# Two up-projection blocks run as one at the entry of a feed-forward layer, with the residual's pieces made on demand

## The chip, the cores and the metric

The kernel runs on one core of one Trainium2 chip. The metric is device time of one execution in microseconds (us), as the median of several runs. Profiles are of one execution.

## The reference

A decoder layer on 256 tokens of width 2048, in float32: two token mixers with a gated merge, cross-attention into 256 memory tokens, and a feed-forward layer with a causal convolution. Each is wrapped in norms. What matters here is the seam between the second and the third:

```python
x = x + rms_norm(cross_attention(h, m, ...), xattn_post_norm[l])
h = rms_norm(x, ffn_pre_norm[l])
x = x + rms_norm(conv_glu_ffn(h, ffn_w_up[l], ...), ffn_post_norm[l])

def conv_glu_ffn(h, w_up, conv_w, conv_b, w_down):
    u = h @ w_up                                    # 2048 x 16384
    uc = conv_b + sum(conv_w[j] * shift_right(u, CONV_WIDTH - 1 - j) for j in range(CONV_WIDTH))
    gate, up = split_cols(uc, (D_FF, D_FF))
    return (jax.nn.gelu(gate, approximate=True) * up) @ w_down
```

## The kernel before

**Products in three parts.** Activations lie with features on the 128 partitions and the 256 tokens along the free axis: `x` is 16 tiles (k) of 128 x 256. Each operand of a large product is split into a rounded high part and the rest (`hi`, `lo`), and a product is three matmuls: high weight by high input, high weight by low input, low weight by high input (L432 to L434: `wh` with `xh`, `wh` with `xl`, `wl` with `xh`).

**Blocks and chunks.** The weights are read once, as chunks of 512 KB (128 x 1024 f32). `Feed` (L320) takes each chunk through three steps: SP loads it into `raw` (L335, three buffers), ACT makes `wh` (L360, four buffers), DVE makes `wl` (L381, four buffers). `run` (L393) goes through a list of blocks in order. A block of the up-projection is 512 columns: 8 chunks, each with two k-tiles and four groups of 128 columns, so 24 matmuls a chunk and 192 a block. It accumulates in two PSUM banks, which its evacuation (`fu_evac`, L1491) later turns into 2 x 128 rows of the gated activation `ac`. There are 32 such blocks (L1539), and two pools of four banks, `acc` and `aux`.

**The order of the work.** Every engine executes its instructions in the order written. `run` writes, at chunk i: a round of side work (`side.half`), the request for the input tile (`b["xs"](k)`, L421), `wh` and `wl` up to chunk i+3 (`feed.lo(i + 3)`, L422), the load up to chunk i+6, and then the matmuls. Side work (evacuations, statistics, transposes) is given as generators to `Spread` (L71), which advances them piece by piece within a budget of ACT and DVE time; `need` and `until` advance a generator at once.

**The residual.** Between two sublayers `Residual` (L1214) makes the new `x` and the next input. Its row of factors comes from the sum of squares of the previous output (`st`, `stb`: small matmuls on PE). Then come eight pieces of two tiles each: on DVE `z` times the factors (`scale`) and `xr` plus `z` (`add`), on ACT the high part `fh`, on DVE the low part `fl` (`parts`). The first piece works tile by tile (256 columns), the others on both tiles (512 columns), one step ahead: `scale` and `add` of piece i+1 stand in front of `parts` of piece i. It is a generator too. In the feed-forward layer it stands in the budgeted list, and `tile(k)` (L1294) also asks for three pieces from the start, always two beyond the one of tile k. Cross-attention uses the same class with `early=True` and the names `qh`, `ql`. After piece 6 the squares of the new `x` are summed (`stf`), for the factors which the evacuation applies; the `xt` transposes (L1571) start with the first evacuation.

Of the kernel before, what the change touches and what calls it, by code (L numbers as in the profile page):

```python
# [15 lines left out]
P = 128  # L16
D = 2048
S = 256
# [52 lines left out]
class Spread:  # L71
# [23 lines left out]
    def add(self, gen, chain=0, phase=0, back=False, ahead_of=None):  # L95
        s = {"gen": gen, "done": False, "gap": chain, "next": self.tick + phase}
        if ahead_of in self.back:
            self.back.insert(self.back.index(ahead_of), s)
        else:
            (self.chains if chain else self.back if back else self.bulk).append(s)  # L100
        return s

    def half(self):
        self.tick += 1
# [42 lines left out]
def _layer(ctx, tc, nc, d, dbg):  # L147
    act, dve = Meter(nc.scalar, 200.0, 0.83), Meter(nc.vector, 130.0, 1.04)
    pool, pe, sp = nc.gpsimd, nc.tensor, nc.sync
    side = Spread(act, dve)  # L150
# [30 lines left out]
    def mm(out, lhsT, rhs, start=True, stop=True):  # L181
        pe.matmul(out, lhsT, rhs, start=start, stop=stop, skip_group_check=True)  # L182
# [128 lines left out]

    blocks = []

    def block(kind, srcs, xs, evac, before=None, cols=512, pool_=None, pre=None, bankwise=False, tail=0):

        blocks.append(dict(kind=kind, srcs=srcs, xs=xs, evac=evac, before=before, cols=cols,
                           pool=pool_ or acc, pre=pre, task=None, bankwise=bankwise, tail=tail))
        return blocks[-1]

    class Feed:  # L320
# [72 lines left out]
    def run():  # L393
        feed = Feed()
        for c in range(8):
            x_load(c)
            feed.dma(c)
        i = 0
        pend = []
        for b in blocks:  # L400
            if len(pend) >= 2:
                side.need(pend[-2])
            if b["before"]:
                b["before"]()
            nm = b["cols"] // P
            if b["kind"] == "fm":
                banks = [b["pool"]("fm", [P, 2, S]) for _ in range((nm + 1) // 2)]
            else:
                banks = [b["pool"]("tm") for _ in range(2 * (b["cols"] // 512))]
            nk = sum(s.shape[1] for s in b["srcs"])  # L410
            k = 0
            nt = len(b["srcs"]) if b["bankwise"] else b["tail"]
            if nt:
                b["srcs"], tail = b["srcs"][:-nt], b["srcs"][-nt:]
            for ci, s in enumerate(b["srcs"]):
                if b["pre"]:
                    b["pre"](ci, feed)
                feed.lo(i + 1)
                side.half()
                side.more = lambda: feed.hi(i + 2)  # L420
                ahead = b["xs"](k)  # L421
                feed.lo(i + 3)  # L422
                feed.dma(i + 6)
                wh, wl = feed.st.pop(i)
                for kj in range(s.shape[1]):
                    xh, xl = b["xs"](k) if kj else ahead
                    first, last = k == 0, k == nk - 1
                    if b["kind"] == "fm":
                        for m in range(nm):
                            o = banks[m // 2][:, m % 2]  # L430
                            a, c = wh[:, kj, m * P:(m + 1) * P], wl[:, kj, m * P:(m + 1) * P]
                            mm(o, a, xh, start=(first and m % 2 == 0), stop=False)  # L432
                            mm(o, a, xl, start=False, stop=False)
                            mm(o, c, xh, start=False, stop=last)  # L434
                            if nm == 8 and m == 3:
                                side.half()
                    else:
                        for g, o in enumerate(banks):
                            tm_products(o, g * P * 512 // b["cols"], g * 512 % b["cols"], (wh[:, kj], wl[:, kj], xh, xl),
                                        first, last)  # L440
                            if len(banks) == 4 and g == 1:
                                side.half()
                    k += 1
                    if kj + 1 < s.shape[1]:
                        side.half()
                i += 1
            if nt:

                feed.lo(i + nt - 1)
                steps = []  # L450
                for s in tail:
                    w = feed.st.pop(i)
                    for kj in range(s.shape[1]):
                        steps.append((w[0][:, kj], w[1][:, kj]) + tuple(b["xs"](k)))
                        k += 1
                    i += 1
                for g, o in enumerate(banks):
                    for si, (wh, wl, xh, xl) in enumerate(steps):
                        if b["kind"] == "tm":
                            tm_products(o, g * P * 512 // b["cols"], g * 512 % b["cols"], (wh, wl, xh, xl), False,  # L460
                                        si == len(steps) - 1)
                        for m in range(2 if b["kind"] == "fm" else 0):
                            c = slice((g * 2 + m) * P, (g * 2 + m + 1) * P)
                            mm(o[:, m], wh[:, c], xh, start=(b["bankwise"] and si == 0 and m == 0), stop=False)
                            mm(o[:, m], wh[:, c], xl, start=False, stop=False)
                            mm(o[:, m], wl[:, c], xh, start=False, stop=si == len(steps) - 1)
                        if si % 2:
                            side.half()
                    if g == 0:
                        feed.lo(i + 1)  # L470
                feed.dma(i + 4)
            b["task"] = side.add(b["evac"](banks))
            pend.append(b["task"])
# [740 lines left out]
    class Residual:  # L1214


        def __init__(self, st, key, st2, hi, lo, gname, early):
            self.a = (st, key, hi, lo, gname)
            self.early, self.stats = early, None
            self.st2, self.ready = st2, 0  # L1220
            self.task = side.add(self.run(), chain=2 if early else 0)

        def run(self):
            st, key, hi, lo, gname = self.a
            z, xr = M[key], M["xr"]
            for _ in range(10):
                if st.done:
                    break
                yield
            while not st.done:  # L1230
                side._piece(side.bulk[0])
            if not self.early:
                keep_warm(2)
            rb = st.row()
            if not self.early:
                keep_warm(4)

            def parts(i, js=(0, 1)):
                for j in js:
                    k = i * 2 + j  # L1240
                    act.activation(hi[:, k], part(xr, i)[:, j], AF.Identity, scale=pcol(gname, k))
                for j in js:
                    k = i * 2 + j
                    dve.scalar_tensor_tensor(lo[:, k], part(xr, i)[:, j], pcol(gname, k), hi[:, k],
                                             op0=ALU.mult, op1=ALU.subtract)
                self.ready = i + 1

            def scale(i):
                dve.tensor_mul(part(z, i), part(z, i), bc(rb, 2))

            def add(i):
                dve.tensor_add(part(xr, i), part(xr, i), part(z, i))

            if self.early:
                yield
            a, x = part(z, 0), part(xr, 0)
            for j in range(2):
                dve.tensor_mul(a[:, j], a[:, j], rb)
            for j in range(2):
                dve.tensor_add(x[:, j], x[:, j], a[:, j])  # L1260
            scale(1)
            parts(0)
            yield
            for i in range(1, 8):
                if i == 1:
                    add(1)
                if i < 7:
                    scale(i + 1)
                    add(i + 1)
                parts(i)  # L1270
                if i == 1 and not self.early:
                    side.more()
                if i == 6:
                    self.stats = side.add(self.squares(), chain=1)
                yield
# [16 lines left out]
            side.need(self.stats)  # L1292

        def tile(self, k):  # L1294
            n = min(k // 2 + 3, 8)
            side.until(self.task, lambda: self.ready >= n)
            return self.a[2][:, k], self.a[3][:, k]

# [237 lines left out]
            return M["res"].tile(k)  # L1536
        return xs

    for b in range(32):  # L1539
        fu = block("fm", W("w_fu", b), fu_xs(b), fu_evac(b),  # L1540
              before=start_ffn if b == 0 else None, pool_=aux if b == 2 else acc)

    M["as"] = {}

# [197 lines left out]
```

## Time and profile before

| what | value |
|---|---|
| median of three runs | 1906.09 us (1905.71 to 1906.88) |
| the profiled execution | 1904.21 us |
| its span, first to last instruction | 1902.4 us |
| granted clock of TensorE | 0.999 |
| L381 DVE `wl`, 640 times | 1224 ns each |
| L360 ACT `wh`, 640 times | 1048 ns each |
| PE matmuls on `fh`, `fl` (up-projection) | 3 x 2048 |
| loads of `w_fu` | 256 of 512.0 KB, 4.2 us to landing (median) |

PE is TensorE's matmuls and PEld its weight loads, DVE VectorE, ACT ScalarE, POOL GpSimd; SP issues the loads. Rows of a timeline give start, duration, engine, line, operation, output and inputs, and in brackets the idle time of the engine before the row and what ended it. Rows of the windows give length, and busy time and instruction count of each engine. Matmuls overlap in the pipe: a row of 0.28 us is followed by the next one's start after 0.11 us.

### The profile page before, as it was taken

What the parts mean: (1) busy time and instruction counts of PE and PEld (TensorE: products, weight loads), DVE (VectorE), ACT (ScalarE), POOL (GpSimd) and SP (SyncE); (2) the same over time, 40 slices, a digit from 0 to 9 for tenths busy, and PEclk for the clock granted to TensorE, in tenths of its full rate; (3) what the DMA queues carried; (4) which work ended last, traced back from release to release, by engine and by line L of the source; (5) the groups of instructions that cost most, each with busy time, mean ns of one, the idle gap of its engine ahead of it and who ended that gap; (6) DMA issues with size and microseconds to landing.
All of it is one profiled execution on the core that took longest, in us unless ns stands there. A gap on an engine that the chain in (4) does not pass through costs nothing.

```text
span 1902.4 us, 36482 instructions
## 1 busy us (share of the span) xinstructions
PE 1881.1 (99%) x15076; PEld 1780.3 (94%) x15076; DVE 1304.6 (69%) x1836; ACT 999.7 (53%) x1438; POOL 32.1 (2%) x53
## 2 busy tenths in 40 slices
PE   9999999999999999989999999999999999999998
PEld 9999987999999999789999999999999998888886
DVE  6888975665765767678666776666776675556555
ACT  6676355544544655566555554545544454555453
POOL 0100000100100000000000000000000000000000
PEclk9999999999999999999999999999999999999999
DMA  7655554354556664536556655665556666555554
GB/s 249 183 183 181 167 163 144 110 169 144 182 178 203 234 239 167 166 117 195 192 189 194 195 189 193 197 196 192 188 193 200 194 194 212 193 197 195 193 190 154
DMA packets 97910, 352.72 MB, mean 185 GB/s; under 512 B 11056, under 2 KB 11312, under 8 KB 97360
## 3 DMA queue, kind: packets, MB, share of 16 engines
q1 hardware_dynamic: 96496, 348.07, 56.2%
q8 instruction: 118, 1.93, 0.4%
q0 software_dynamic: 384, 1.18, 0.3%
q10 hardware_dynamic: 864, 1.15, 0.2%
q14 instruction: 48, 0.39, 0.1%
HBM read 347.73 MB, written 2.10 MB: 184 GB/s over the span
## 4 chain that ended last, share of the span: by engine, by line
PE 93%; DVE 3%; DMA 2%; ACT 1%; issue 1%; POOL 0%; DVEq 0%; POOLq 0%; ACTq 0%
PE fm L182 65%; PE tm L182 24%; DVE wl L381 1%; DMA raw<-in_w_in_dram 1%; PE gram L182 0%; PE Y L182 0%; PE lv L182 0%; DVE fl L66 0%; ACT wh L360 0%; DMA x<-in_x_dram 0%; PE num L182 0%; DVE z L66 0%; PE U L182 0%; PE X L182 0%; PE zwa L182 0%
## 5 line engine op out<-in xcount | busy, mean ns | idle before, releaser
L381 DVE TENSOR_TENSOR wl<-raw,wh 128x1024 fp32r<-128x1024 f32 x640 | 779.6, 1224 | 437.0 <-ACT wh L360 434.6
L360 ACT CAST wh<-raw 128x1024 fp32r<-128x1024 f32 x640 | 669.2, 1048 | 526.2 <-PE fm L182 367.5
L182 PE MATMUL fm<-fh,wl 128*128 128x256 f32 x2048 | 566.3, 277 | 2.6 <-DVE wl L381 2.6
L182 PE MATMUL fm<-fh,wh 128*128 128x256 f32 x2048 | 567.1, 277 | 1.3 <-ACT fh L66 0.8
L182 PE MATMUL fm<-fl,wh 128*128 128x256 f32 x2048 | 566.2, 276 | 0.4 <-DVE fl L66 0.4
L182 PEld LDWEIGHTS fm<-fh,wl 128*128 128x128 f32 x2048 | 384.8, 188 | 3.2 <-DVE wl L381 3.2
L182 PEld LDWEIGHTS fm<-fh,wh 128*128 128x128 f32 x2048 | 384.7, 188 | 1.6 <-ACT fh L66 1.0
L182 PEld LDWEIGHTS fm<-fl,wh 128*128 128x128 f32 x2048 | 384.7, 188 | 0.8 <-DVE fl L66 0.8
L182 PE MATMUL tm<-wh,as 128*128 128x512 f32 x1024 | 315.2, 389 | 0.0
L182 PE MATMUL fm<-hh,wh 128*128 128x256 f32 x1072 | 302.7, 282 | 1.2 <-ACT wh L371 1.2
L182 PE MATMUL fm<-hh,wl 128*128 128x256 f32 x1072 | 298.3, 278 | 1.7 <-DVE wl L381 1.5
L182 PE MATMUL fm<-hl,wh 128*128 128x256 f32 x1072 | 297.9, 278 | 0.0
L182 PEld LDWEIGHTS tm<-wh,as 128*128 128x128 f32 x1024 | 192.2, 188 | 39.9
L182 PEld LDWEIGHTS fm<-hh,wh 128*128 128x128 f32 x1072 | 201.8, 188 | 3.9 <-ACT hh L66 1.5
L182 PEld LDWEIGHTS fm<-hh,wl 128*128 128x128 f32 x1072 | 201.7, 188 | 2.7 <-DVE wl L381 2.4
L182 PEld LDWEIGHTS fm<-hl,wh 128*128 128x128 f32 x1072 | 201.8, 188 | 0.2
L182 PE MATMUL tm<-wl,as 128*128 128x512 f32 x512 | 199.2, 389 | 0.0
L182 PEld LDWEIGHTS tm<-wl,as 128*128 128x128 f32 x512 | 96.1, 188 | 19.8
L66 ACT CAST as<-ac 128x256 fp32r<-128x256 f32 x128 | 45.6, 404 | 111.7 <-PE tm L182 111.7
L66 DVE TENSOR_TENSOR as<-ac,as 128x256 fp32r<-128x256 f32 x128 | 48.6, 421 | 60.8 <-ACT as L66 60.8
L182 PE MATMUL fm<-mgh,wh 128*128 128x256 f32 x256 | 71.1, 278 | 0.0
L182 PE MATMUL fm<-mgh,wl 128*128 128x256 f32 x256 | 70.9, 277 | 0.0
(363 smaller groups left out, 2147.8 us busy)
## 6 DMA issues: line engine op xcount, KB each, us to landing
raw<-in_w_fu_dram SPq DMA_DIRECT2D x256, 512.0 KB, 4.2
raw<-in_w_in_dram SPq DMA_DIRECT2D x160, 512.0 KB, 3.6
raw<-in_w_fd_dram SPq DMA_DIRECT2D x128, 512.0 KB, 4.2
raw<-in_w_br_dram SPq DMA_DIRECT2D x32, 512.0 KB, 3.9
raw<-in_w_mo_dram SPq DMA_DIRECT2D x32, 512.0 KB, 4.0
raw<-in_w_xk_dram SPq DMA_DIRECT2D x8, 512.0 KB, 4.4
raw<-in_w_xq_dram SPq DMA_DIRECT2D x8, 512.0 KB, 3.6
raw<-in_w_xv_dram SPq DMA_DIRECT2D x8, 512.0 KB, 4.2
```

The source lines that it names most:

```text
L66: return f(out, *a, **k)
L182: pe.matmul(out, lhsT, rhs, start=start, stop=stop, skip_group_check=True)
L360: nc.scalar.copy(wh, r)
L381: nc.vector.tensor_sub(wl, r, self.st[self.nl][0])
```

## The change

The first two blocks of the up-projection become one block of 16 chunks, which alternate between the two: chunk 0 of block 0, chunk 0 of block 1, chunk 1 of block 0, and so on. It holds four banks and is evacuated once, block 0 first (`fu_evac2`). For the very first k-tile the four products with the low part of the input come after the eight others. The feed-forward residual leaves the budgeted list: only `tile(k)` advances it, and it asks for one piece beyond the one of tile k instead of two. In both residuals the first piece alternates `mul` and `add` by tile, and its high and low parts stand ahead of `scale(1)`.

```diff
+    def own(self, gen):
+
+        return {"gen": gen, "done": False}
...
-                banks = [b["pool"]("fm", [P, 2, S]) for _ in range((nm + 1) // 2)]
+                banks = [b["pool"]("fm", [P, 2, S]) for _ in range((nm + 1) // 2 * (1 + b["two"]))]
...
-            nk = sum(s.shape[1] for s in b["srcs"])
+            nk = sum(s.shape[1] for s in b["srcs"]) // (1 + b["two"])
...
             for ci, s in enumerate(b["srcs"]):
+                second = b["two"] and ci % 2
+                if second:
+                    k -= s.shape[1]
...
                         for m in range(nm):
-                            o = banks[m // 2][:, m % 2]
+                            o = banks[second * 2 + m // 2][:, m % 2]
                             a, c = wh[:, kj, m * P:(m + 1) * P], wl[:, kj, m * P:(m + 1) * P]
                             mm(o, a, xh, start=(first and m % 2 == 0), stop=False)
-                            mm(o, a, xl, start=False, stop=False)
+                            if not (b["two"] and ci == 0 and first):
+                                mm(o, a, xl, start=False, stop=False)
                             mm(o, c, xh, start=False, stop=last)
-                            if nm == 8 and m == 3:
-                                side.half()
+                        if b["two"] and ci == 0 and first:
+
+                            for m in range(nm):
+                                mm(banks[m // 2][:, m % 2], wh[:, kj, m * P:(m + 1) * P], xl, start=False, stop=False)
...
-            self.task = side.add(self.run(), chain=2 if early else 0)
+            if early:
+                self.task = side.add(self.run(), chain=2)
+            else:
+                self.task = side.own(self.run())
...
             for j in range(2):
                 dve.tensor_mul(a[:, j], a[:, j], rb)
-            for j in range(2):
                 dve.tensor_add(x[:, j], x[:, j], a[:, j])
+            parts(0)
             scale(1)
-            parts(0)
             yield
...
         def tile(self, k):
-            n = min(k // 2 + 3, 8)
+            n = min(k // 2 + (3 if self.early else 2), 8)
             side.until(self.task, lambda: self.ready >= n)
...
+    def fu_evac2(ps):
+        for b in range(2):
+            yield from fu_evac(b)(ps[b * 2:b * 2 + 2])
+
+    block("fm", [w for c in zip(W("w_fu", 0), W("w_fu", 1)) for w in c], fu_xs(0), fu_evac2, before=start_ffn, two=True)
+    for b in range(2, 32):
+        fu = block("fm", W("w_fu", b), fu_xs(b), fu_evac(b), pool_=aux if b == 2 else acc)
```

`nm` is four in all these blocks, so the removed `side.half` was never reached.

More of the change, by code (lines that the diff above doesn't have):

```diff
@@ L312, in _layer, with block @@
     blocks = []
-    def block(kind, srcs, xs, evac, before=None, cols=512, pool_=None, pre=None, bankwise=False, tail=0):
+    def block(kind, srcs, xs, evac, before=None, cols=512, pool_=None, pre=None, bankwise=False, tail=0,
+              two=False):
         blocks.append(dict(kind=kind, srcs=srcs, xs=xs, evac=evac, before=before, cols=cols,
-                           pool=pool_ or acc, pre=pre, task=None, bankwise=bankwise, tail=tail))
+                           pool=pool_ or acc, pre=pre, task=None, bankwise=bankwise, tail=tail, two=two))
         return blocks[-1]
@@ L1537, in fu_xs @@
         return xs
-    for b in range(32):
-        fu = block("fm", W("w_fu", b), fu_xs(b), fu_evac(b),
-              before=start_ffn if b == 0 else None, pool_=aux if b == 2 else acc)
+    def fu_evac2(ps):
[4 more added lines that the diff above has]
+        fu = block("fm", W("w_fu", b), fu_xs(b), fu_evac(b), pool_=aux if b == 2 else acc)
     M["as"] = {}
```

## The prediction

> **What bounds the kernel now.** I read the page first, then the windows around the entry of the up-projection and the chain of waits there, then the timelines of PE, DVE and ACT.
>
> ```profile
> PE 1881.1 (99%) x15076; PEld 1780.3 (94%) x15076; DVE 1304.6 (69%) x1836; ACT 999.7 (53%) x1438; POOL 32.1 (2%) x53
> ...
> PE 93%; DVE 3%; DMA 2%; ACT 1%; issue 1%; POOL 0%; DVEq 0%; POOLq 0%; ACTq 0%
> ```
>
> PE is busy 99% of the span and carries 93% of the chain that ends last, so only PE's matmuls and the few places where it waits can be worth anything. The 3% of DVE in the chain is the clue: somewhere PE follows DVE. The windows give blocks 0 and 1 of the up-projection, and block 6 as the standard (length, then busy time and count of PE, PEld, DVE, ACT, POOL, then clock, DMA share, GB/s):
>
> ```profile
> 837.24:864.61 27.37, 23.91 (x192) 22.76 (x193) 26.85 (x44) 18.56 (x31) 0.00 (x0) 1.00 0.37 119
> 864.61:889.10 24.49, 24.11 (x211) 23.94 (x210) 18.27 (x27) 14.19 (x18) 0.70 (x1) 1.00 0.59 195
> ...
> 979.24:1001.01 21.77, 21.77 (x195) 21.77 (x193) 15.11 (x21) 10.90 (x14) 0.00 (x0) 1.00 0.59 195
> ```
>
> A block is 192 matmuls, 8 chunks of 24 (counts take in two or three from the edges). It takes 21.77 us when nothing stops it: 0.1134 a matmul, 2.72 a chunk. Block 0 takes 27.37, with DVE busy for 26.85 of it; block 1 takes 24.49. Together 51.86 against 43.54: **8.32 us over**. At the entry DVE is the bound: it owes one piece of the residual and one `wl` per chunk.
>
> PE's timeline shows where the 8.32 goes:
>
> ```profile
> 837.24 0.38 PE L182 MATMUL fm<-fh,wh 128*128 128x256 f32 x1 [0.83 <-ACT fh L66]
> 838.02 0.38 PE L182 MATMUL fm<-fl,wh 128*128 128x256 f32 x1 [0.40 <-DVE fl L66]
> ...
> 844.39 0.38 PE L182 MATMUL fm<-fh,wl 128*128 128x256 f32 x1 [0.53 <-DVE wl L381]
> ...
> 850.89 0.39 PE L182 MATMUL fm<-fh,wl 128*128 128x256 f32 x1 [0.44 <-DVE wl L381]
> ...
> 854.10 0.38 PE L182 MATMUL fm<-fh,wh 128*128 128x256 f32 x1 [0.43 <-ACT wh L360]
> ...
> 856.26 0.38 PE L182 MATMUL fm<-fh,wl 128*128 128x256 f32 x1 [1.66 <-DVE wl L381]
> ...
> 867.97 0.58 PE L182 MATMUL st<-ones,stf 128*128 128x1 f32 x4 [0.38 <-DVE stf L66]
> ```
>
> and the chain of waits has the small matmuls of block 1:
>
> ```profile
> 867.97 0.58 PE st L182 x4
> ...
> 871.47 0.44 PE stb L182 x4
> ...
> 874.75 0.44 PE xt L1581 x4
> ...
> 886.08 0.44 PE xt L1581 x4
> ```
>
> The five waits inside block 0 (0.40, 0.53, 0.44, 0.43, 1.66) add to 3.46. Each costs more than its bracket: from 837.24 to 838.02 PE loses 0.78 - 0.11 = 0.67, 0.27 over the bracket, since a row is drawn longer than the spacing; and the matmul after a restart is another 0.11 late. So 3.46 + 5 x 0.38 = **5.4 us**. `st`, `stb` and two `xt` take 0.58 + 3 x 0.44 = 1.9, and `st` waits 0.38 besides. That leaves 0.6: a slightly wider spacing of the matmuls.
>
> ```profile
> 856.60:864.96 8.36, 8.36 (x73) 1.00 0.65 213
> 1002.00:1010.36 8.36, 8.36 (x76) 1.00 0.54 182
> ```
>
> In windows of one length, at full clock and without an idle slot, 73 matmuls stand where 76 stand later: 4% of 2.72, 0.11 us a chunk. The wide spacing runs from the restart at 856.26 to the first `xt`.
>
> **The change part by part.** The profiled execution took 1904.21 us (span 1902.4 and 1.8 around it), 1.9 under the median 1906.09. I work out the difference inside the span and take it from the median.
>
> *Chunks in turn.* Blocks 0 and 1 become 16 chunks, so each piece (two k-tiles) feeds two chunks, 5.44 us of PE. DVE's rows at the entry give its prices:
>
> ```profile
> 835.55 0.75 DVE L66 TENSOR_TENSOR z<-z,stb 128x256 f32<-128x256 f32 x2 [1.58 <-PE stb L182]
> 836.22 0.75 DVE L66 TENSOR_TENSOR xr<-xr,z 128x256 f32<-128x256 f32 x2
> 836.89 0.68 DVE L66 TENSOR_TENSOR z<-z,stb 128x512 f32<-128x512 f32 x1
> 837.49 0.88 DVE L66 SCALAR_TENSOR_TENSOR fl<-xr,par,fh 128x256 fp32r<-128x256 f32 x2
> 838.28 0.69 DVE L66 TENSOR_TENSOR xr<-xr,z 128x512 f32<-128x512 f32 x1
> 838.88 0.68 DVE L66 TENSOR_TENSOR z<-z,stb 128x512 f32<-128x512 f32 x1
> 839.60 0.69 DVE L66 TENSOR_TENSOR xr<-xr,z 128x512 f32<-128x512 f32 x1
> 840.21 0.87 DVE L66 SCALAR_TENSOR_TENSOR fl<-xr,par,fh 128x256 fp32r<-128x256 f32 x2
> 841.00 0.68 DVE L66 TENSOR_TENSOR z<-z,stb 128x512 f32<-128x512 f32 x1
> ...
> 843.12 2.35 DVE L381 TENSOR_TENSOR wl<-raw,wh 128x1024 fp32r<-128x1024 f32 x2
> 845.39 0.68 DVE L66 TENSOR_TENSOR z<-z,stb 128x512 f32<-128x512 f32 x1
> ```
>
> A piece is 838.88 to 841.00, 2.12; a `wl` is (845.39 - 843.12)/2 = 1.14. Before: 2.12 + 1.14 = 3.26 per chunk against PE's 2.72, so PE has to stall. After: 2.12 + 2 x 1.14 = 4.40 per 5.44. DVE has 1.04 to spare in each pair of chunks, if its work comes in the right order.
>
> *Order at the entry.* `z` and `xr` now alternate by half tile. A step that reads what the step just before it wrote starts 0.72 after it (838.88 to 839.60), an independent one 0.61 (839.60 to 840.21): 0.11 more. Independent 256-wide steps stand 0.335 apart (0.67 for two). So: z 835.55, xr 836.00, z 836.33, xr 836.78 (ending 837.19), `fl` from 837.11.
>
> ```profile
> 836.67 0.91 ACT L66 ACTIVATE fh<-xr,par 128x256 fp32r<-128x256 f32 x2 [2.62 <-DVE xr L66]
> ...
> 839.82 1.03 ACT L360 CAST wh<-raw 128x1024 fp32r<-128x1024 f32 x1
> ```
>
> `fh` began 0.45 after its `xr` (836.22), PE 0.57 after that. Now `fh` begins at 836.45 and PE at 837.02, **0.2 earlier**. The eight products without `fl` come first and last to 838.0, and `fl` is there at 837.6: the wait at 838.02 goes. The second half of `fh` starts only at 837.2 and ends at 837.7, so DVE loses another 0.26 before the second `fl`. It is free at 838.17 with `z` of piece 1 still to do; its `xr` follows at 838.9, 0.6 later than before.
>
> [...]
>
> *Every deadline.* In the changed program DVE does p0, p1, `wl2` `wl3` `wl4`, p2, `wl5` `wl6`, p3, `wl7` `wl8`, p4 and so on (p is a piece; chunks 0 and 1 are staged already). Adding the prices: p1 ends at 841.7, `wl2` 842.85, `wl3` 844.0, `wl4` 845.1, p2 847.2. PE begins chunk 1 at 839.85, 2 at 842.6, 3 at 845.3, 4 at 848.0, then each 2.72. `wl2` is wanted 0.23 into chunk 2, at 842.8: a tie, for which I take 0.2 (between 0 and the 0.53 + 0.38 of the wait at 844.39, nearer to 0). `wl3` and `wl4` are 1.5 and 3 early, p2 0.8.
>
> *The weights' transfers.* There are three raw buffers, so a transfer starts when the `wl` three chunks before it ends. First SP's waits, then the transfers issued at 844.40 and at 845.50, each in a window of its own:
>
> ```profile
> SPq L335 <- DVE wl L381: 47.1, 14, 13.4
> ```
> ```profile
> raw<-in_w_fu_dram SPq DMA_DIRECT2D x1, 512.0 KB, 3.5
> ```
> ```profile
> raw<-in_w_fu_dram SPq DMA_DIRECT2D x1, 512.0 KB, 4.3
> ```
>
> SP waits for DVE 14 times. Of two transfers 1.1 apart the first lands in 3.5, the second in 4.3, 1.9 after the first. Chunk 5's now starts at 842.9 and lands at 846.4, chunk 6's at 844.0 to 848.3, chunk 7's at 845.1 to 850.2, later ones in 4.3. With 1.03 for `wh` and 1.2 for `wl`: `wl5` ends at 848.8, `wl6` 850.7, p3 852.8, `wl7` 853.9, `wl8` 855.4, p4 857.5, `wl9` 858.6, `wl10` 860.5, p5 862.6. PE wants chunk 5 at 851, p3 at 853.7, p4 at 859.1, p5 at 864.5: at least 0.9 early each time. **No further stall.** ACT has 2 x 1.03 + 0.91 in 5.44 and hides.
>
> *What only moves.* `st` now stands behind 396 matmuls instead of 216, with `stb` and the `xt` after it; the counts stay, so their 1.9 is paid later, in full. The `st` wait of 0.38 should go: the fold of `stf` follows `wl18`, due more than a chunk before. The evacuations of both blocks now run together, from chunk 18 on. One is 15.11 - 8 x 1.14 = 6.0 of DVE, and each later block leaves DVE 21.77 - 15.11 = 6.7 idle, so two blocks hide the one that is behind. I cost it at nothing; without that cover it is up to 6.0.
>
> *The first residual* (cross-attention) gets the same new order, under a saturated DVE:
>
> ```profile
> 737.92 0.87 DVE L66 SCALAR_TENSOR_TENSOR ql<-xr,par,qh 128x256 fp32r<-128x256 f32 x2
> 738.98 1.23 DVE L381 TENSOR_TENSOR wl<-raw,wh 128x1024 fp32r<-128x1024 f32 x1 [0.19 <-ACT wh L360]
> ```
> ```profile
> PE st L182 <- DVE stx L66: 1.5, 1, 1.5
> ```
>
> Two dependent steps and the wait for `fh` delay it by 0.5; the idle 0.19 takes up part. Between 0 and 0.5 reaches the `st` for which PE already waits 1.5. I take 0.2, near 0.5 less the idle and the `wh` that shifts with it.
>
> **Sum.** Gains: 5.4, 0.4 (`st`), 0.2 (start). Costs: 0.2 (first residual), 0.1 (the restart after the first matmul), 0.2 (chunk 2). The wide spacing cost 0.6; it may now cost 0 to 1.7 (16 chunks at 0.11), and I take 0.7. Net **5.4 us**: 1904.2 - 5.4 = 1898.8 for the profiled execution, **1900.7** as a median. What follows is PE's work and shifts as a whole.
>
> **The rivals.** (1) *Transfers land late together.* If the three in flight share the bandwidth evenly, 1.57 MB at the 195 GB/s of block 1's row last 8.1 us, and all land near 851. Then `wl5` is ready at 853.2 instead of 851 and p3 is pushed 0.5 past its chunk; with restarts 3 us of the gain go: 1903.7. Against it stand the 3.5 and 4.3 above. [...]
>
> (2) *The tie of chunk 2 returns at each pair.* The pieces are in truth not made only when asked for: one is queued a pair ahead, in front of the next `wl`, on an engine that works in order. Seven times 0.6 is 4.2: gain 1.2, time 1904.9. For it: the small margin of p2, 0.8. Against: DVE gains 1.04 each pair.
>
> (3) *Slower: the wide spacing stays.* Without stalls nothing interrupts PE until `st`. If PE keeps the spacing of 856 to 865, it pays 0.11 a chunk: from 55 chunks on the gain is gone, from 90 on the kernel is slower by 0.2%, and over all 256 chunks of the up-projection it is 28 us, 1928. For it: before, it lasted 18 us and through `st` and `stb`. Against: it ended at an `xt`, eight groups of `xt` follow here too, and block 6 shows no trace of it.
>
> **How the numbers follow.** The forecast has 0.70, from 1899.4 (no wide spacing, no tie) to 1902.3 (both in full); transfers 0.15; ties 0.09; spacing 0.06. A measurement of this kernel tells about 0.2%, 3.8 us, from no change: the forecast is faster by more than that (below 1902.3), (1) and (2) lie within it, (3) is slower. So faster 0.70, same 0.24, slower 0.06. The range, 1899.2 to 1904.2, takes in (1) and leaves out (2) and (3).
>
> **What would show it.** Right: the first matmul 1.5 us after the first `z` (1.7 now); the merged block's 384 matmuls in 44 to 45.5 us; no wait of PE on `wl` over 0.5, none on `fl`; `st` without a wait; `xt` still 32. (1) would show as ACT's `wh` waiting for DMA and PE for `wl` near 851; (2) as six or seven waits of PE on `wl` or `fl` at even chunks; (3) as 73 matmuls instead of 76 in 8.36 us late in the up-projection. I am wrong at the root if PE, free of DVE here, loses the time again before block 6.

## The result and the profile after

The changed kernel takes **1900.48 us** in the median of six executions, the kernel before on the same chip 1907.22. One of the six took 3822.03 us at a granted clock of 1.0, for a reason that nothing here shows, and is left out of the ratio: **0.9964 [0.9954, 0.9975]**, which is 6.9 us faster (4.8 to 8.8). The profiled execution took 1898.43 us (span 1896.7) against 1904.21 (1902.4), so 5.78 less in the two profiles.

The page of the kernel after, its busy times and the shares of the chain that ended last:

```profile
PE 1879.7 (99%) x15076; PEld 1780.6 (94%) x15076; DVE 1305.0 (69%) x1836; ACT 1000.2 (53%) x1438; POOL 32.1 (2%) x53
...
PE 93%; DVE 3%; ACT 2%; issue 1%; DMA 1%; POOL 0%; SPq 0%; DVEq 0%; POOLq 0%; ACTq 0%
```

The counts of matmuls and of DVE's and ACT's instructions are the same, and DVE's busy time differs by 0.4 us: no work went, it was put in another order. The 3% of DVE in the chain hardly answer, because 6 us are 0.3% of a span and the shares are rounded to whole per cents. The stage itself answers. Windows of the kernel after: blocks 0 and 1 as one (384 matmuls from the first), then blocks 2 to 5 with what moved into them, then block 6 as the standard (length, busy time and count of PE, PEld, DVE, ACT, POOL, then clock, DMA share, GB/s):

```profile
837.22:881.26 44.04, 44.04 (x384) 43.89 (x385) 40.20 (x56) 27.91 (x40) 0.00 (x0) 1.00 0.59 189
881.26:973.35 92.09, 92.09 (x811) 92.09 (x809) 66.29 (x96) 51.97 (x71) 0.70 (x1) 1.00 0.58 185
973.35:995.11 21.76, 21.76 (x194) 21.76 (x193) 15.03 (x21) 10.90 (x14) 0.00 (x0) 1.00 0.59 194
```

and the row of the kernel before for its blocks 2 to 5:

```profile
889.10:979.24 90.14, 90.14 (x794) 90.14 (x793) 60.84 (x82) 46.74 (x62) 0.00 (x0) 1.00 0.60 191
```

In the first row PE's busy time equals the length: it doesn't stop once. The two blocks took 51.86 before and take 44.04 now, 7.82 less. The next stretch takes 92.09 instead of 90.14, 1.95 more, with 17 matmuls more in it (four rows of four, and one at the edge): `st`, `stb` and two `xt` were inside blocks 0 and 1 and now stand behind them. DVE does 5.45 us more there, the evacuation that was put off, and PE's busy time is still equal to the length. So 7.82 - 1.95 = 5.87, and 0.02 from the start (837.22 against 837.24): block 6 begins at 973.35 instead of 979.24, **5.89 earlier**. The last matmul of the up-projection ends the same 5.89 earlier.

The chain of waits of the kernel after, at the entry and at the end of the merged block, shows the same without the sums:

```profile
835.74 0.43 DVE z L66
836.18 0.02 issue
836.20 0.44 DVE xr L66
836.64 0.02 issue
836.66 0.52 ACT fh L66
837.18 0.04 issue
837.22 45.56 PE fm L186 x396
882.78 0.34 PE st L186 x4
883.12 2.94 PE fm L186 x24
886.06 0.44 PE stb L186 x4
886.50 2.75 PE fm L186 x24
889.25 0.44 PE xt L1599 x4
```

One `z`, one `xr`, one half of `fh`, then 396 matmuls in a single step of the chain: nothing of DVE stands between them any more. `st` follows directly, with no wait.

The groups of the page that read `fh`, before and after (out<-in, shapes and count, then busy time, mean ns of one, then idle time of PE just before them and its releaser), say it for the whole up-projection. After:

```profile
L186 PE MATMUL fm<-fh,wl 128*128 128x256 f32 x2048 | 565.8, 276 | 0.0
L186 PE MATMUL fm<-fh,wh 128*128 128x256 f32 x2048 | 566.6, 277 | 0.6 <-ACT fh L66 0.6
L186 PE MATMUL fm<-fl,wh 128*128 128x256 f32 x2048 | 565.3, 276 | 0.0
```

The 0.6 is the first matmul's wait for `fh`; ahead of no other product of the up-projection's blocks is PE idle. One wait is too short to show as idle time of PE: the weight loads (PEld) of the products on `wl` wait for it for 0.2 us in all, which is the tie at chunk 2 below.

### The profile page after: what moved, and what is told of

The parts are those of the page before. It is cut to its first block, busy times and chain, and to the rows that moved or that the text cites. A ratio compares the mean times of both kernels' runs of the same rounds, so it can differ in the third digit from the quotient of the medians.

```text
span 1896.7 us, 36486 instructions
## 1 busy us (share of the span) xinstructions
PE 1879.7 (99%) x15076; PEld 1780.6 (94%) x15076; DVE 1305.0 (69%) x1836; ACT 1000.2 (53%) x1438; POOL 32.1 (2%) x53
## 4 chain that ended last, share of the span: by engine, by line
PE 93%; DVE 3%; ACT 2%; issue 1%; DMA 1%; POOL 0%; SPq 0%; DVEq 0%; POOLq 0%; ACTq 0%
PE fm L186 65%; PE tm L186 24%; DVE wl L387 1%; ACT wh L366 1%; PE gram L186 0%; PE Y L186 0%; PE lv L186 0%; DMA raw<-in_w_in_dram 0%; DVE ql L66 0%; DMA wsm<-in_w_sm_dram 0%; DVE z L66 0%; PE num L186 0%; PE U L186 0%; ACT hh L66 0%; PE X L186 0%
```

## The experiments

The theory: **DVE's load per matmul of PE** decides. At the entry DVE owed 3.26 us for each 2.72 of PE, and taking chunks in turn makes it 4.40 for each 5.44; but only if DVE also *does* its work in that order, for which the demand is needed. The rivals: the order alone, or the demand alone, or the new order of the first piece is the real cause. The first four kernels take the parts apart, the next three load DVE to find the point at which it decides, and the last changes one detail at the entry. What is moved to later blocks is paid there, so besides blocks 0 and 1 I give the time from the first matmul to the start of block 6: 142.00 us in the kernel before (27.37 + 24.49 + 90.14), 136.13 in the changed one (44.04 + 92.09), with the same matmuls in it everywhere.

**1. Chunks in turn, alone** (residual, its requests and the order of its first piece as before; the `block` lines are against the kernel before, the `if` against the changed one)

```diff
+    block("fm", [w for c in zip(W("w_fu", 0), W("w_fu", 1)) for w in c], fu_xs(0), fu_evac2, before=start_ffn, two=True)
+    for b in range(2, 32):
...
-                            if not (b["two"] and ci == 0 and first):
+                            if True:
                                 mm(o, a, xl, start=False, stop=False)
...
             self.task = side.add(self.run(), chain=2 if early else 0)
...
             n = min(k // 2 + 3, 8)
```

> Blocks 0 and 1 interleaved as in the changed kernel, all else as before: the residual in the budgeted list, three pieces from the start, old order of the first piece and of the first products. Theory (what counts is the order in which DVE gets its work, and the interleaving only makes room for it): in the program DVE's steps stand exactly as before (p0 p1 p2, wl2 wl3, p3 p4, wl4, p5 p6, wl5, p7, wl6), so wl4 and wl5 end when they ended before, 850.9 and 856.2, and PE, which reaches chunks 4 and 5 at 848.0 and 853.6 now, waits for them as before. The 384 matmuls take about 51 us less the st, stb and xt that moved out (1.9 and 0.4): 49 to 49.5. Time within 1 us of before. Rival (interleaving alone feeds PE): the 384 matmuls in 44 to 45 us and 5 us faster.

Measured: 1907.55 against 1905.93, ratio 1.0006 [0.9996, 1.0016]. Windows of this kernel, its blocks 0 and 1 in halves:

```profile
839.23:866.31 27.08, 23.30 (x193) 22.31 (x193) 26.36 (x43) 18.14 (x31) 0.00 (x0) 1.00 0.36 116
866.31:891.25 24.94, 24.07 (x207) 23.89 (x205) 14.57 (x16) 9.88 (x10) 0.70 (x1) 1.00 0.66 212
```

Together 52.02, as before (51.86), with 12 small matmuls in it instead of 16: only one group of `xt` moved out. `st` did not move behind the two blocks, as I had assumed, since the residual was finished as early as before; it waits 0.9 for `stf` in this kernel. Up to block 6 it is 142.70, which is 0.70 more than before. PE merely waits for other things. Rows of its timeline:

```profile
852.88 0.38 PE L186 MATMUL fm<-fh,wl 128*128 128x256 f32 x1 [0.77 <-DVE wl L387]
...
856.09 0.39 PE L186 MATMUL fm<-fh,wh 128*128 128x256 f32 x1 [0.43 <-ACT wh L366]
...
858.25 0.38 PE L186 MATMUL fm<-fh,wl 128*128 128x256 f32 x1 [1.66 <-DVE wl L387]
```

The last is the 1.66 of the kernel before, to the digit. DVE's instructions are the same ones in the same order: three pieces, two `wl`, then twice two pieces and one `wl`. PE needs half as many pieces in a block, but DVE makes them at the old rate all the same, in front of the `wl` that PE is waiting for. **The order of the chunks alone is worth nothing.**

**2. The demand, alone** (blocks 0 and 1 apart)

```diff
-            self.task = side.add(self.run(), chain=2 if early else 0)
+            if early:
+                self.task = side.add(self.run(), chain=2)
+            else:
+                self.task = side.own(self.run())
...
-            n = min(k // 2 + 3, 8)
+            n = min(k // 2 + (3 if self.early else 2), 8)
```

> Only the residual on demand: out of the budgeted list, two pieces from the start, one ahead of need; blocks 0 and 1 one after the other and the old order of the first piece and first products. Theory: DVE still owes 3.26 us per chunk against PE's 2.72, but the wl now alternate with the pieces (p0 p1 wl2 wl3 p2 wl4 p3 wl5 ... wl8 p7), so the waits become small and many and the last is p7's, at 835.55 + 8 x 2.12 + 7 x 1.14 + 0.1 = 860.6, where PE began chunk 7 at 861.8 before. Block 0 takes 25.5 to 26.5 us instead of 27.4; 1 to 2 us faster than before. Rival (making pieces on demand is the gain): block 0 in 22 to 23 us and 5 us faster.

Measured: 1904.70 against 1905.93, 0.9993 [0.9984, 1.0003], a difference that the interval doesn't separate from none. The windows of blocks 0 and 1, and PE's waits in block 0 (in total, times, longest):

```profile
837.13:863.48 26.35, 23.75 (x192) 22.55 (x193) 26.04 (x42) 18.18 (x30) 0.00 (x0) 1.00 0.45 142
863.48:886.89 23.41, 23.41 (x207) 23.41 (x205) 16.20 (x23) 12.87 (x17) 0.70 (x1) 1.00 0.61 192
```
```profile
PE fm L186 <- DVE fl L66: 2.6, 6, 1.4
PE fm L186 <- ACT fh L66: 0.8, 1, 0.8
```

Block 0 is 26.35 instead of 27.37, DVE busy for 26.04 of it, which is 8 x 3.26 = 26.1. The waits on `wl` have become waits on `fl`: pieces and weights keep their prices, and DVE is still the bound in block 0. Block 1 has no wait and one group of `xt` less. Up to block 6 it is 140.37, which is 1.63 less than before.

**3. The new order of the first piece, alone** (`mul` and `add` in turn, its parts ahead of `scale(1)`, the products with `fl` last)

```diff
...
                 dve.tensor_mul(a[:, j], a[:, j], rb)
-            for j in range(2):
                 dve.tensor_add(x[:, j], x[:, j], a[:, j])
-            scale(1)
             parts(0)
+            scale(1)
```

> Only the order at the entry: mul and add alternate by half tile in the first piece of both residuals with its parts ahead of scale(1), and the first k-tile's low-input products come after the eight others; blocks one after the other, residual in the budgeted list. Theory: PE starts 0.2 earlier and has no wait at its second matmul, but DVE falls 0.6 behind and every later wait of PE is on DVE, so the 0.9 comes back at chunk 2 and wl5 ends 0.6 later; with 0.2 in cross-attention the kernel is 0.6 to 1 us slower. Rival (the entry's order is part of the gain by itself): 0.9 us faster.

Measured: 1907.91 against 1905.93, 1.0011 [1.0001, 1.0020]: slightly slower. Block 0 takes 29.53. A new wait stands in chunk 1, in PE's timeline:

```profile
843.26 0.38 PE L182 MATMUL fm<-fl,wh 128*128 128x256 f32 x1 [0.79 <-DVE fl L66]
```

The wait for `wl` of chunk 5 ended 20.71 us after the first `z` before and ends 21.33 after it here: 0.62 later, which is the 0.6 by which the prediction said that DVE falls behind at the entry. The rest of the 2.2 was not expected; windows of PE alone show it (length, PE, clock, DMA share, GB/s):

```profile
854.00:858.70 4.70, 2.66 (x22) 1.00 0.34 112
858.70:859.80 1.10, 1.04 (x8) 0.95 0.21 41
859.80:863.20 3.40, 3.40 (x18) 0.51 0.80 259
863.20:870.00 6.80, 6.80 (x61) 1.00 0.62 193
```

For 3.4 us the granted clock is 0.51, with 18 matmuls where 30 fit at 0.1134. That is 12 x 0.113 = 1.4 us. So this profile shows the theory's 0.6 and a loss by the clock that I had not forecast; how much of the slower median is the clock, the times don't tell.

**4. All but the new order of the first piece** (the edits of 1 and 2 together)

> The changed kernel without its order at the entry: interleaved blocks and the residual on demand, but the old order of the first piece in both residuals and of the first products. Theory: PE starts 0.2 later and waits 0.7 at its second matmul, but DVE is 0.6 ahead, so chunk 2 has no wait, and cross-attention is 0.2 shorter: 384 matmuls in 44.3 to 44.8 us, 0.2 to 0.7 us slower than the changed kernel, some 5 us faster than before. Rival (the order at the entry carries a good part): 1.5 us or more slower than the changed kernel.

Measured: 1901.47 against 1905.93, 0.9974 [0.9964, 0.9983]. Windows of its two halves:

```profile
841.23:864.62 23.39, 22.98 (x193) 22.79 (x193) 21.03 (x30) 13.63 (x20) 0.00 (x0) 1.00 0.55 179
864.62:886.47 21.85, 21.85 (x194) 21.85 (x193) 18.71 (x26) 14.22 (x20) 0.00 (x0) 1.00 0.60 191
```

Together 45.24, which is 6.62 under before, and less the 1.95 that is paid later 4.67. Nearly the whole gain is here, from two edits of which alone, up to block 6, one lost 0.70 us and the other gained 1.63. **They need each other**: the chunks in turn make room on DVE, and the demand lets the `wl` use it. The changed kernel's 44.04 is 1.2 less. Of it 0.67 is the second matmul's wait for `fl`, and 0.75 is spacing: here the 192 matmuls of chunks 0 to 7 stand 0.1178 apart instead of 0.1134, in the changed kernel they don't. Against it stand 0.23 at chunk 2, where this kernel has no wait. The spacing is what puts 45.24 over the 44.3 to 44.8 that I had expected. The medians (0.9974 and 0.9964, intervals overlapping) don't separate this 1.2.

**5. The changed kernel with the low part made twice** in pieces 2 to 7: 0.79 more on DVE per pair of chunks, the same values written again

```diff
+                for j in js * (0 if self.early or i < 2 else 1):
+                    k = i * 2 + j
+                    nc.vector.scalar_tensor_tensor(lo[:, k], part(xr, i)[:, j], pcol(gname, k), hi[:, k],
+                                             op0=ALU.mult, op1=ALU.subtract)
```

> The changed kernel; DVE computes the low part of pieces 2 to 7 of the feed-forward residual twice (0.79 us more a piece, the same values), so a pair of chunks asks 5.19 of DVE against PE's 5.44. Theory (DVE's share of a pair is what decides): it still fits; where DVE waited for weights it works instead, and the 384 matmuls take 44.0 to 44.6 us, the time within 1 us of the changed kernel. Rival (the margin is in truth used up by the transfers and the small lead of the pieces): a wait of PE at each pair, 384 matmuls in 47 us or more.

Measured: 1901.54 against 1906.89, 0.9971 [0.9962, 0.9981]. Its two halves:

```profile
841.07:863.32 22.25, 22.25 (x193) 22.25 (x193) 21.61 (x35) 12.68 (x18) 0.00 (x0) 0.98 0.51 163
863.32:885.25 21.93, 21.93 (x194) 21.93 (x193) 21.55 (x33) 15.20 (x23) 0.00 (x0) 1.00 0.62 192
```

DVE is busy for 43.16 of 44.18 us, and PE still doesn't stop. 4.40 + 0.79 = 5.19 is under 5.44: in the merged block the work is free. The clock of 0.98 is a stretch at half clock around the first two matmuls (838.45 to 841.86), which costs 0.38 and hides the 0.23 at chunk 2; that is the 0.14 over 44.04. Up to block 6 it is 136.76, 0.63 more than in the changed kernel, since the matmuls around `st` come 0.36 later.

**6. The same, four times** (`js * 3`: 2.37 more per pair)

> The changed kernel; the low part of pieces 2 to 7 computed four times (2.37 us more a piece), so a pair asks 6.77 of DVE against 5.44 of PE. Theory: DVE is the bound again. Adding the prices from the first wl on, piece 6 ends 6.7 us after PE wants it and piece 7 another 2 later: 384 matmuls in 52 to 55 us, 8 to 11 us slower than the changed kernel, PE's waits on fl. Rival (the DVE load does not decide): under 3 us slower.

Measured in one execution: 1910.75. Windows of its halves, and the first of PE's waits from there to 900 us:

```profile
840.02:864.69 24.67, 22.88 (x193) 22.36 (x193) 24.31 (x43) 12.31 (x18) 0.00 (x0) 1.00 0.43 142
864.69:892.22 27.53, 23.02 (x195) 22.23 (x193) 27.15 (x48) 14.54 (x23) 0.00 (x0) 1.00 0.46 144
```
```profile
PE fm L186 <- DVE fl L1263: 6.3, 6, 1.7
```

DVE now owes 4.40 + 2.37 = 6.77 per 5.44, 1.33 too much, six times: 8.0. The two halves take 52.20, which is 8.16 more than in the changed kernel. The six waits stand at the first matmul on the new piece in chunks 4, 6, 8, 10, 12 and 14: the prediction's second rival, brought about by added work. Behind the block `st` waits another 1.2 for `stf`, and up to block 6 it is 145.85, 9.72 more than in the changed kernel.

**7. The kernel before with the low part made twice** (the edit of 5, in the kernel before)

> The kernel before with the low part of pieces 2 to 7 computed twice (0.79 us more a piece). Theory: here DVE is the bound, so what the changed kernel hides is paid in full: five pieces stand before wl5, 3.95 us, and one more before wl6. Block 0 takes 31.3 to 32.2 us instead of 27.4, or up to 1.7 more where the long waits bring the clock down as they did in the run with the entry's order alone. Rival (PE is held by its own restarts or by the transfers): block 0 under 29 us.

Measured in one execution: 1911.54. Block 0:

```profile
840.03:872.88 32.85, 25.79 (x193) 24.40 (x193) 32.33 (x56) 19.02 (x32) 0.00 (x0) 0.95 0.35 105
```

5.48 more than the 27.37 of before, for 6 x 0.79 = 4.74 of DVE's work, and half the clock again (0.50 for 3.3 us), which by the working of experiment 3 is about 1.4 of the 5.48. So some 4.1 are left for the 4.74, near the 3.95 of the five pieces that stand ahead of the last wait on `wl`. What costs nothing in 5 costs most of its price here.

**8. The changed kernel, `scale(1)` between the two halves of the first piece's parts**, in the feed-forward layer; cross-attention as before

```diff
-            parts(0)
-            scale(1)
+                parts(0, (0,))
+                scale(1)
+                parts(0, (1,))
```

> The changed kernel with two small differences: at the entry the scale of piece 1 stands between the two halves of the first low part, so DVE does not wait for the second half of the high part (0.26 less, and 0.1 for the dependent step), and cross-attention's residual has its old order. Theory: wl2 ends 0.3 to 0.4 sooner, the 0.23 lost at chunk 2 goes, 384 matmuls in 43.7 to 43.9 us; cross-attention 0 to 0.3 shorter. In all 0.2 to 0.6 us faster than the changed kernel, less than the times can tell. Rival (the tie at chunk 2 comes from the weights' high part or from elsewhere): the 0.2 stays.

Measured: 1901.86 against 1906.89, 0.9976 [0.9965, 0.9988]. Windows:

```profile
838.33:860.36 22.03, 22.03 (x192) 21.95 (x193) 20.18 (x30) 13.38 (x20) 0.00 (x0) 1.00 0.53 167
860.36:882.29 21.93, 21.93 (x194) 21.93 (x193) 19.97 (x27) 14.60 (x22) 0.00 (x0) 1.00 0.66 213
```

43.96 instead of 44.04: the tie at chunk 2 is gone, but the second half of `fl` is now 0.15 late at the fourteenth matmul. That is just over the 43.7 to 43.9 that I had expected, and the 0.2 to 0.6 by which it was to be faster can't be seen. Little is left to win here: 384 matmuls at 0.1134 are 43.54. A fourth buffer for the raw weights was not tried.

## Why the prediction was right, point by point

**What bounds.** Blocks 0 and 1 took 8.32 us more than two standard blocks, most of it by DVE's load. Experiments 5, 6 and 7 show that cause: DVE's added work is free while its sum per pair lies under 5.44, and in experiment 6 it is paid in full over it. My 5.4 for the five waits was 0.4 too much: from one matmul's start to the next, only the first wait costs 0.38 over its bracket, the other four 0.27, since that already holds the late matmul behind the restart. The five are 4.9. A tie in chunk 3 without a bracket, where two matmuls stand 0.237 and 0.226 apart, is another 0.24; the rest is the small matmuls with the wait of `st`, 2.4, and spacing, 0.7. The forecast is hardly touched by it, since all of the waits go.

**The entry.** I said 1.5 us from the first `z` to the first matmul, before 1.69: it is 837.22 - 835.74 = 1.48. DVE's timeline of the kernel after shows the rest:

```profile
837.34 0.48 DVE L66 SCALAR_TENSOR_TENSOR fl<-xr,par,fh 128x256 fp32r<-128x256 f32 x1
838.00 0.48 DVE L66 SCALAR_TENSOR_TENSOR fl<-xr,par,fh 128x256 fp32r<-128x256 f32 x1 [0.18 <-ACT fh L66]
838.40 0.68 DVE L66 TENSOR_TENSOR z<-z,stb 128x512 f32<-128x512 f32 x1
...
841.84 3.49 DVE L387 TENSOR_TENSOR wl<-raw,wh 128x1024 fp32r<-128x1024 f32 x3
845.25 0.68 DVE L66 TENSOR_TENSOR z<-z,stb 128x512 f32<-128x512 f32 x1
...
847.82 1.23 DVE L387 TENSOR_TENSOR wl<-raw,wh 128x1024 fp32r<-128x1024 f32 x1 [0.37 <-ACT wh L366]
...
849.74 1.23 DVE L387 TENSOR_TENSOR wl<-raw,wh 128x1024 fp32r<-128x1024 f32 x1 [0.70 <-ACT wh L366]
...
853.00 2.35 DVE L387 TENSOR_TENSOR wl<-raw,wh 128x1024 fp32r<-128x1024 f32 x2
```

The whole entry stands 0.19 later in this profile than in that of before (`z` at 835.74 instead of 835.55). With that shift the forecast has DVE free at 838.36 (it is 838.40), the three `wl` from 841.9 (841.84), piece 2 from 845.3 (845.25), `wl7` from 853.0 (853.00). The wait of DVE for the second half of `fh` is the [0.18] (I said 0.26). The alternation cost what I had taken from the rows of 0.61 and 0.72: the first `xr` starts 0.46 after the `z` that it reads (835.74 to 836.20), against 0.45 in the forecast. Deadlines added from rows of the kernel before thus held to 0.1 us over 17 us, because the changed order has no step of a kind that the old trace lacks.

**The tie at chunk 2.** Taken at 0.2; two matmuls there stand 0.231 and 0.222 apart instead of 0.1134, 0.23 together. It did not return at later pairs.

**The transfers.** Three issues, at 843.09, 844.22 and 845.36 (I said 842.9, 844.0 and 845.1, before the shift of 0.19), each in a window of its own, with the time to landing in the last column:

```profile
raw<-in_w_fu_dram SPq DMA_DIRECT2D x1, 512.0 KB, 3.5
```
```profile
raw<-in_w_fu_dram SPq DMA_DIRECT2D x1, 512.0 KB, 4.3
```
```profile
raw<-in_w_fu_dram SPq DMA_DIRECT2D x1, 512.0 KB, 4.6
```

They land one after the other, at 846.6, 848.5 and 850.0, and not together near 851 as the rival had it: the first rival did not come. ACT and DVE wait for them (the [0.37] and [0.70] above are `wl` behind `wh` behind these loads); PE does not.

**What only moves.** 1.9 for `st`, `stb` and two `xt`: 1.95. The `st` wait of 0.38 went. The postponed evacuation, taken at 6.0 of DVE under PE's cover, is the 5.45 above, without a stall.

**The first residual.** Taken at 0.2. From its `z` to the `st` of cross-attention it is 37.63 us in the mean of six profiles with the old order (37.34 to 37.89) and 37.91 in four with the new one (37.64 to 38.04): 0.28, with a scatter about as large. In line with 0.2, and only just resolved.

**The term that was mis-sized** is the wide spacing, taken at 0.7 for the merged block: it did not come. Only the 24 matmuls of chunk 8 stand wide, 0.120 apart: 0.16. That explains the gain of 5.89 instead of 5.4; the sum of what is left over the 43.54 is 0.11 (the restart) + 0.23 + 0.16 = 0.50, and 44.04 - 43.54 = 0.50.

And chunk 8 is another thing than the spacing of the prediction. The program (`staged`) puts the weights of chunks 8, 24, 40, 56, 72, 120, 184 and 248 of the up-projection at element 24 of their tile and those of its other chunks at element 16. In all ten profiles the matmuls of chunks 24 to 248 of this list stand 0.120 apart, and those of no other chunk do; those of chunk 8 do so in six profiles. So this spacing goes with the place of the weights, and the kernel before pays it too. The spacing of 0.1178 comes behind some restarts of PE and not behind others (in the second experiment in chunks 2 and 4, not in 3 and 5). In the fourth experiment it lasted from the start to chunk 8 and ended there. What sets it stays open. The third rival, in which it stays and makes the kernel slower, did not come: blocks 2 to 5 take 1.95 more than before, of which the moved small matmuls are 1.9, and block 6 takes 21.76 against 21.77.

**The total.** Predicted 5.4 off the profile of before; the profiles differ by 5.78, and the ratio's interval of 4.8 to 8.8 us holds both. The 6.9 of the ratio is more than the entry explains, but not resolvably so. That the median came within 0.2 of the forecast is partly luck: the kernel before came out at 1907.22 and not at the 1906.09 that I had built on, and the difference of the medians, 6.7, is 1.3 more than my 5.4. The lower end of the band with 0.70 was added up wrongly: without the wide spacing and the tie my terms give 1899.8, not 1899.4.

## What to carry to other kernels

When two engines share a stage and the helper owes more per unit than the main one has time for, look for work of the helper that is made once and can be used twice before more is asked of it; here each piece of the residual feeds two chunks instead of one. Such a reordering is worth nothing until the helper's own program order changes with it: budgeted or early-queued work keeps its old place in front of what is due, so the two edits gave -0.7 and 1.6 us alone and 4.7 together. Add up the helper's prices per round and compare with the main engine's time for that round: here, while the sum stayed under it (5.19 us of 5.44), added work cost nothing, and over it (6.77) the excess was paid (8.16 us in six rounds).

## What was not expected of the hardware

**Half the clock behind waits like those of the kernel before.** In the third and seventh experiments the granted clock fell to half for 3.4 us inside block 0 (0.51 and 0.50 in their windows). The windows of PE alone in the seventh:

```profile
859.50:864.20 4.70, 1.45 (x11) 0.99 0.09 18
864.20:867.50 3.30, 3.30 (x18) 0.50 0.65 199
867.50:872.00 4.50, 4.50 (x40) 1.00 0.64 203
```

Here PE had been busy for 1.45 of 4.7 us, with one wait of 3.25. In the third it had been busy for 2.66 of 4.7, with waits of 0.44 and 1.67. The kernel before has two waits of the same size at that place, 0.43 and 1.66, and kept its full clock behind them (1.00 from 856.20 to 863.00), so these waits alone don't decide it.

The clock's records in the traces show more. Inside the program every stretch at half clock lasts 3.413 us, and the full clock between two of them lasts a whole number of times that long (7 and 17 times in the seventh experiment). The full clock up to the fall behind the last matmul, 1894.397 us in the kernel before and 1880.744 in the changed one, is 555 and 551 times 3.4133. So the changes in these records stand on a grid of this step. Take the step of the grid that ends where the clock falls: PE was busy in it for 1.43 of 3.41 us in the third experiment (856.28 to 859.70) and for 1.05 in the seventh (860.66 to 864.07). The emptiest steps of these blocks without a fall behind them are 1.70 in the sixth (884.65 to 888.06), 1.76 in the first (856.27 to 859.69, with the same two waits as before) and 1.99 in the kernel before (854.84 to 858.25). My estimate from these five is that the same waits can cost the clock or not, by how they lie on the grid. It fits all the falls inside the two blocks, but no experiment set it, and it gives no limit: at the start of the kernel after, the clock fell at 7.88 us behind a step in which PE was busy for 1.75.

Other falls in the first 11 us and behind the last matmul aside, the clock also fell near 776 us, behind the wait of cross-attention's `st`, in experiments 4 to 7 (0.94 to 1.57 us busy in the step ahead) and in none of the other six profiles (2.0 or more), and at the entry itself in the fifth (838.45) and seventh (836.77). There the step ahead is drawn busy for 2.62 and 2.94, much of it by small matmuls, and the estimate above doesn't explain it. Inside the merged block of the changed kernel PE has no pause and the clock is 1.00; the pause ahead of its first matmul stays, and the fifth experiment, which is the changed kernel with added work, lost its clock there.

**The start of the entry scatters.** The first matmul of the up-projection stood between 837.1 and 841.2 us in the profiles of these kernels, and that does not come from the entry. At the first `zwa` matmul the ten profiles already lie between 83.0 and 85.3 us, and they keep these distances to within 0.1 up to 727 us. Then the four with the half clock near 776 lose about 1.8 more (33.8 to 34.0 us from the first `qh` product to the first `xsc`, 31.6 to 32.4 in the others), and these four are the ones that start the up-projection at 840.0 or later. So a difference of a microsecond between two single profiles is better read from the stage that was changed than from the end of the span.
